# First products of a decoder layer taken by k-tile over both token tiles, with x loaded in smaller pieces

## The chip, the core and the metric

The kernel runs on one core of a Trainium2 chip. The metric is the time of one execution on the device in microseconds (us); a lower time is better. Five engines run their own instruction lists side by side and wait for each other through semaphores: TensorE (PE, matrix products; PEld is its loading of the stationary operand), VectorE (DVE), ScalarE (ACT), GpSimd (POOL) and SyncE (SP, which here only issues DMA transfers). Each list is worked through in the order in which it was written.

## What is computed

One layer of a decoder over 256 tokens of width 1024 in float32: a half-step feed-forward block with SwiGLU, two token mixers that share one input projection, and a second half-step feed-forward block, each followed by a layer norm. The part that matters here is the first feed-forward block:

```python
def swiglu(x, w_up, w_down):
    gate, up = jnp.split(x @ w_up, 2, axis=-1)
    return (jax.nn.silu(gate) * up) @ w_down

x = layer_norm(ALPHA * x + 0.5 * swiglu(x, ffn1_w_up[l], ffn1_w_down[l]), ln1_g[l], ln1_b[l])
```

x is 256 x 1024, w_up is 1024 x 5632 and w_down is 2816 x 1024.

## The kernel before

**Products in three passes.** Each float32 operand is split into a high part of type fp32r (a cast, on ACT) and a low part, the operand less its high part (a subtraction, on DVE). A product of a k-tile (128 rows of the contraction) is three matmuls that add up in one bank of PSUM: high x high, high of x with low of w, low of x with high of w. `passes` (L119) writes these three, and all of them are recorded on L117.

**Tokens** come in two tiles of 128 rows, t = 0 and t = 1. x has to stand transposed for the products: a block of 128 x 128 is transposed by TensorE (L190) into a bank of PSUM, four blocks to a bank, and `split` takes high (L203, ACT) and low (L204, DVE) out of that bank into the tile `X`. `XT(key, t, src, half)` does this for one token tile and half of the 1024 columns.

**Weights** come in units of 1 MB. A unit has a `raw` tile, which the DMA fills (L865), and two tiles `S` for its high part (cast on ACT, L875) and low part (subtraction on DVE, L878). There are three `raw` buffers, and the load of a further unit waits until the last low part of the unit that held its buffer is made. The first two units, columns 0 to 255 of gate and up for all of k, are loaded and split in four chunks of 128 x 512 each: a chunk is one k-tile, so unit 0 holds k = 0 to 3 and unit 1 holds k = 4 to 7. Later units are split in two chunks of 128 x 1024.

**The first products** are the 48 matmuls that `rows_both` (L316) writes: 8 k-tiles x 3 passes x 2 token tiles into one bank for each token tile. The order is half by half and in each half token tile by token tile: k = 0 to 3 of t = 0, k = 0 to 3 of t = 1, then k = 4 to 7 of t = 0 and of t = 1. The transposes of x stand ahead of them and between them: x of t = 0, columns 0 to 511, first; after 6 products x of t = 1, columns 0 to 511; after 12 and 18 products the two other halves. When a bank is full, `U_epi` takes it on (Silu on ACT, L391, and a product on DVE, L392). Behind the 48 stand the column units (`U_cols`), in which the weights are the stationary operand: eight products of 512 columns with the high part, of which the first four read the unit's first chunk, and eight of 256 columns with the low part.

**Ahead of the products** TensorE multiplies zeros from the tile `still`: `idle(6)` before the first transposes and `idle(3)` after them (L147).

**What sets the order.** All engines' lists are written by one walk over TensorE's operations (L913 on), which keeps a clock of its own, one column of a product at 1/2400 us. Before each operation `advance` (L890) decides whether chunks of weights are split now: a chunk that the operation's unit needs is always written first, whole unit by whole unit; further chunks when their due time is less than a lead ahead, no sooner after the chunk before than a pace allows, and not in a `quiet` time. `prep` (L870) writes the cast on ACT and the subtraction on DVE. What follows an operation (the split of a bank of transposes, Silu) is written right behind it, so casts of weights and casts of x stand on ACT's list in the order of this walk.

**Loads.** `load` (L860) issues the transfers of the weights on SP. Between the chunks of unit 0 it puts x: chunks 0 and 1, then x of t = 1 columns 0 to 511, chunks 2 and 3, then the two other halves of x. x of t = 0, columns 0 to 511, is issued by ACT as its first instruction.

## Time and profile before

| | us |
|---|---|
| median of three runs | 647.35 (646.94 to 647.46) |
| the profiled execution | 647.14 |
| its span, from the first to the last instruction | 645.1 |
| PE busy | 635.1, 3440 matmuls |
| DVE busy | 449.9 |
| ACT busy | 354.8 |

A profile has one row for an instruction, or for a run of equal ones (x6 is six of them, and the duration then goes from the start of the first to the end of the last). Times are counted from the span's start. The bracket at the end of a row says how long the engine stood idle before it and what ended that. Matmuls overlap: the next one starts before the row of the last has ended, so that the distance of their starts is the time that one costs. The span and the time outside it (2.0 us) make the time of the execution.

### The profile page before, as it was taken

The numbers are of one execution on the slowest core, as the hardware profiler recorded it, in microseconds if no ns is written. First come the engines' busy times: TensorE is split into PE (matmuls) and PEld (weight loads), VectorE is DVE, ScalarE is ACT, GpSimd is POOL, SyncE is SP. The second block draws the span as 40 slices with busy tenths as digits, with TensorE's granted clock in tenths as the row PEclk, the third lists the DMA queues.
The fourth block names the chain that finished last, engine by engine and source line by source line (L and its number), as shares of the span: only waits on it lengthen the run. The fifth ranks groups of instructions, "written<-read, shape, count | busy, mean of one in ns | idle before, by whom it ended". The sixth has DMA issues, their size and how long they took to land.

```text
span 645.1 us, 8783 instructions
## 1 busy us (share of the span) xinstructions
PE 635.1 (98%) x3440; PEld 548.6 (85%) x3440; DVE 449.9 (70%) x707; ACT 354.8 (55%) x608; POOL 18.6 (3%) x27
## 2 busy tenths in 40 slices
PE   8999999999999999999999999999999999999995
PEld 6888888888888888898888888888888888888884
DVE  4776666656678676777659898886866666666636
ACT  5665555555534558667678665552555555555510
POOL 2000000000011000000000000001100000000002
PEclk9999999999999999999999999999999999999999
DMA  8866666668636573546647656572565755555301
GB/s 292 284 207 199 221 226 202 199 203 274 193 113 192 156 216 97 185 134 206 186 139 215 234 196 195 196 253 75 195 194 203 257 196 196 196 196 195 131 2 65
DMA packets 95854, 121.18 MB, mean 188 GB/s; under 512 B 2197, under 2 KB 84421, under 8 KB 95813
## 3 DMA queue, kind: packets, MB, share of 16 engines
q1 hardware_dynamic: 95668, 120.36, 57.4%
q8 instruction: 27, 0.44, 0.3%
q10 hardware_dynamic: 144, 0.26, 0.1%
q14 instruction: 15, 0.11, 0.1%
HBM read 119.56 MB, written 1.05 MB: 187 GB/s over the span
## 4 chain that ended last, share of the span: by engine, by line
PE 97%; DMA 1%; POOL 0%; DVE 0%; SPq 0%; issue 0%; ACT 0%; POOLq 0%
PE acc L117 96%; PE acc L190 1%; DMA raw<-in_ffn_w_up 1%; SPq L865 0%; POOL rs L250 0%; POOL nmr L812 0%; DVE S L878 0%; ACT S L875 0%; SPq L106 0%; POOLq L944 0%; POOL N L815 0%; DVE bn L240 0%; DVE N L238 0%; DVE mv L246 0%; PE acc L707 0%
## 5 line engine op out<-in xcount | busy, mean ns | idle before, releaser
L117 PE MATMUL acc<-X,S 128*128 128x512 f32 (+1 forms) x2368 | 420.8, 338 | 0.0
L117 PEld LDWEIGHTS acc<-X,S 128*128 128x128 f32 x2368 | 364.3, 189 | 48.8
L878 DVE TENSOR_TENSOR S<-raw,S 128x1024 fp32r<-128x1024 f32 (+1 forms) x224 | 267.9, 1205 | 40.9 <-ACT S L875 39.7
L875 ACT CAST S<-raw 128x1024 fp32r<-128x1024 f32 (+1 forms) x224 | 227.9, 1035 | 47.3 <-PE acc L117 41.2
L117 PE MATMUL acc<-S,T 128*128 128x512 f32 (+1 forms) x546 | 123.7, 383 | 0.0
L117 PEld LDWEIGHTS acc<-S,T 128*128 128x128 f32 x546 | 100.1, 188 | 19.5
L376 DVE TENSOR_TENSOR T<-T,acc 128x256 f32<-128x256 f32 x124 | 52.0, 419 | 85.4 <-ACT T L375 85.3
L375 ACT COPY T<-acc 128x256 f32<-128x256 f32 x124 | 46.0, 371 | 101.7 <-PE acc L117 100.8
L117 PE MATMUL acc<-S,X 128*128 128x512 f32 x336 | 80.3, 394 | 0.9 <-ACT S L875 0.5
L117 PEld LDWEIGHTS acc<-S,X 128*128 128x128 f32 x336 | 62.1, 188 | 14.4 <-DVE S L878 1.2
L213 ACT CAST T<-T 128x256 fp32r<-128x256 f32 x38 | 15.5, 407 | 23.0 <-DVE T L427 23.0
L203 ACT CAST X<-acc 128x512 fp32r<-128x512 f32 (+1 forms) x24 | 12.4, 516 | 26.9 <-PE acc L190 13.7
L204 DVE TENSOR_TENSOR X<-acc,X 128x512 fp32r<-128x512 f32 (+1 forms) x24 | 14.3, 598 | 14.9 <-ACT X L203 14.9
L421 ACT ACTIVATE T<-T 128x256 f32<-128x256 f32 x38 | 15.9, 419 | 11.6 <-DVE T L376 11.6
L238 DVE SCALAR_TENSOR_TENSOR N<-acc,N 128x512 f32<-128x512 f32 (+1 forms) x13 | 8.4, 643 | 15.8 <-PE acc L117 15.8
L250 POOL TENSOR_TENSOR rs<-ve,mhalf 128x1 f32<-128x1 f32 x6 | 5.8, 964 | 460.5 <-DVE ve L248 460.5
L208 DVE TENSOR_TENSOR T<-T,T 128x256 fp32r<-128x256 f32 x38 | 15.9, 419 | 4.4 <-ACT T L213 4.4
L427 DVE TENSOR_TENSOR T<-T 128x256 f32<-128x256 f32 x38 | 16.2, 425 | 1.3
L376 DVE TENSOR_TENSOR N<-N,acc 128x256 f32<-128x256 f32 x24 | 10.1, 419 | 9.3 <-ACT N L375 9.1
L375 ACT COPY N<-acc 128x256 f32<-128x256 f32 x24 | 8.8, 367 | 8.4 <-PE acc L117 8.2
L203 ACT CAST T<-acc 128x128 fp32r<-128x128 f32 (+1 forms) x20 | 7.0, 350 | 7.8 <-PE acc L190 4.0
L204 DVE TENSOR_TENSOR T<-acc,T 128x128 fp32r<-128x128 f32 (+1 forms) x20 | 7.9, 395 | 4.5 <-ACT T L203 4.5
(71 smaller groups left out, 204.8 us busy)
## 6 DMA issues: line engine op xcount, KB each, us to landing
raw<-in_ffn_w_up SPq DMA_DIRECT2D x38, 1024.0 KB, 5.1
raw<-in_w_in SPq DMA_DIRECT2D x32, 1024.0 KB, 5.5
raw<-in_ffn_w_down SPq DMA_DIRECT2D x22, 1024.0 KB, 4.9
raw<-in_w_proj_attn SPq DMA_DIRECT2D x4, 1024.0 KB, 5.6
raw<-in_w_proj_conv SPq DMA_DIRECT2D x4, 1024.0 KB, 4.9
raw<-in_w_out SPq DMA_DIRECT2D x4, 1024.0 KB, 5.0
raw<-in_ffn_w_up SPq DMA_DIRECT2D x8, 512.0 KB, 5.0
raw<-in_ffn_w_up SPq DMA_DIRECT2D x8, 256.0 KB, 5.4
```

The lines of the kernel that those rows point to most:

```text
L117: return Op(lambda: nc.tensor.matmul(dst(), lhsT=lhsT(), rhs=rhs(), start=start, stop=stop), cols, unit)
L203: nc.scalar.copy(hi, src)
L204: nc.vector.tensor_tensor(lo, src, hi.bitcast(F), op=OP.subtract)
L208: nc.vector.tensor_tensor(lo, src, hi.bitcast(F), op=OP.subtract)
L213: nc.scalar.copy(hi, src)
L238: nc.vector.scalar_tensor_tensor(y[:, c], src, scale, st["ax", t][:, c], op0=OP.mult, op1=OP.add)
L375: nc.scalar.copy(dst, bank[:, 256:512])
L376: nc.vector.tensor_tensor(dst, dst, bank[:, 0:256], op=OP.add)
L421: defer(0.8, lambda: nc.scalar.activation(g[:, 0:256], g[:, 0:256], AF.Silu))
L427: nc.vector.tensor_tensor(g[:, 0:256], g[:, 0:256], g[:, 256:512], op=OP.mult)
L875: nc.scalar.copy(u.hi[:, s], u.raw[:, s])
L878: nc.vector.tensor_tensor(u.lo[:, s], u.raw[:, s], u.hi[:, s].bitcast(F), op=OP.subtract)
```

## The change

`rows_both` gets a written order, `seq`, of products (token tile, k-tile, which passes) and of transposes. The products run k-tile by k-tile, both token tiles at each, so that the k-tiles of unit 0 are used up after 24 products and not after the half of one token tile. Each operation also carries the number of its chunk, and `advance` writes only those chunks ahead of it that it needs, no longer the whole unit. Until the fourth split of x is written, `state["quiet"]` is set to 1e9, which keeps chunks from being written ahead of need; after it, to 0. The first chunk alone is written early, by `more`, behind the second group of idle products.

x comes in five pieces in place of four: columns 0 to 255 of t = 0 by ACT, then, each behind one of the four chunks of unit 0 on SP, columns 256 to 511 of t = 0, columns 0 to 511 of t = 1, and the two other halves. `x_first` takes the place of `XT` for x. The first piece is cast and subtracted by DVE alone (`by_dve`); the second one by ACT and DVE in one step of 2 blocks; the third one in two steps of 2 blocks; the last two in one step of 4 blocks. The idle products are 4 and 2 in place of 6 and 3.

```diff
-    load_x(0, 0, nc.scalar)
+    load_x(0, 0, 2, nc.scalar)
...
+    def x_first(t, k, n, done, evac):
+        def out_(bank):
...
+            evac(lambda i, m: (xT[:, k + i:k + i + m, 0, t, :], xT[:, k + i:k + i + m, 1, t, :],
+                               bank.rearrange("p (k n) -> p k n", k=4)[:, i:i + m]))
+            if done:
+                make_ax(t, st["x", t])
+                N.free()
+        return transposes(lambda i: st["x", t][:, (k + i) * 128:(k + i + 1) * 128], n, out_)
...
-    early = {1: [(1, 0)], 3: [(0, 1), (1, 1)]}
+    early = {0: (0, 2, 2), 1: (1, 0, 4), 2: (0, 4, 4), 3: (1, 4, 4)}
...
-    add(idle(6))
-    add(xts[0, 0])
-    add(idle(3))
-    base[-1].after.append(T.free)
-    e0, e1 = ffn("x", a["ffn1_w_up"][0], a["ffn1_w_down"][0], 1, 1,
-                 {6: [xts[1, 0]], 12: [xts[0, 1]], 18: [xts[1, 1]]}, 3, lambda t: ln_fin(t, 1))
+    def by_dve(part):
+        hi, lo, src = part(0, 2)
+        nc.vector.tensor_copy(hi, src)
+        nc.vector.tensor_tensor(lo, src, hi.bitcast(F), op=OP.subtract)
+    def by_both(part, n=4, w=4):
+        for i in range(0, n, w):
+            split(*part(i, w))
+    def open_up():
+        state["quiet"] = 0.0
+    ALL, HI, LO = ((0, 0), (0, 1), (1, 0)), ((0, 0), (1, 0)), ((0, 1),)
+    state["quiet"] = 1e9
+    add(idle(4))
+    add(x_first(0, 0, 2, False, by_dve))
+    e0 = add(idle(2))
+    base[-1].after += [T.free, lambda: more()]
+    first = x_first(0, 2, 2, False, lambda part: by_both(part, 2, 2))
+    second = x_first(1, 0, 4, False, lambda part: by_both(part, 4, 2))
+    third, fourth = (x_first(t, 4, 4, True, by_both) for t in range(2))
+    fourth[-1].after.append(open_up)
+    seq = [first, (0, 0, HI), (0, 0, LO), (0, 1, HI), second, (0, 1, LO), (1, 0, HI[:1]), (1, 1, HI[:1]), (1, 0, LO), (1, 1, LO),
+           (1, 0, HI[1:]), (1, 1, HI[1:]), (0, 2, ALL), third, (1, 2, ALL), (0, 3, ALL), fourth, (1, 3, ALL)]
+    seq += [(t, k, ALL) for k in range(4, KT) for t in range(2)]
...
-            if must is None or pos[id(must)] < state["prep"]:
+            p = -1 if must is None else pos[id(must)]
+            if p < state["prep"] or p == state["prep"] and part is not None and part < c:
```

ACT's list from its first cast to the first Silu. Names: `raw` to `S` is the high part of a chunk of weights, `acc` to `X` the high part of transposed x, `T` from `acc` the Silu. Before:

```order
L203 CAST X_115<-acc_110 128x4x128
L875 CAST S_122<-raw_88 128x512 x4
L203 CAST X_115<-acc_141 128x4x128
L875 CAST S_154<-raw_96 128x512
L203 CAST X_115<-acc_158 128x4x128
L875 CAST S_154<-raw_96 128x512 x2
L203 CAST X_115<-acc_178 128x4x128
L875 CAST S_154<-raw_96 128x512
L875 CAST S_199<-raw_101 128x1024 x2
L391 ACTIVATE T_217<-acc_132 128x256
```

The four chunks of unit 0 stand in a row, ahead of the second piece of x. The same place after the change:

```order
L916 CAST S_118<-raw_88 128x512
L208 CAST X_112<-acc_122 128x2x128
L916 CAST S_118<-raw_88 128x512
L208 CAST X_112<-acc_135 128x2x128 x2
L916 CAST S_118<-raw_88 128x512
L208 CAST X_112<-acc_157 128x4x128
L916 CAST S_118<-raw_88 128x512
L208 CAST X_112<-acc_176 128x4x128
L916 CAST S_185<-raw_97 128x512 x4
L916 CAST S_217<-raw_102 128x1024
L413 ACTIVATE T_225<-acc_127 128x256
L413 ACTIVATE T_231<-acc_145 128x256
```

Chunks of unit 0 and pieces of x now alternate, and the second chunk of the first column unit (`S_217`) has moved behind both Silus.

TensorE's list from the third group of transposes on (`acc_158` and `acc_157`), to the first products of unit 1. `S_122` and `S_118` are the high part of unit 0, `S_154` and `S_185` that of unit 1, `S_155` and `S_186` its low part. Before:

```order
L190 MATMUL acc_158<-ident,N_82 128x128 x4
L117 MATMUL acc_167<-S_122,X_115 128x512
L117 MATMUL acc_167<-S_123,X_115 128x512
L117 MATMUL acc_167<-S_122,X_115 128x512 x2
L117 MATMUL acc_167<-S_123,X_115 128x512
L117 MATMUL acc_167<-S_122,X_115 128x512
L190 MATMUL acc_178<-ident,N_83 128x128 x4
```

After:

```order
L195 MATMUL acc_157<-ident,N_82 128x128 x4
L118 MATMUL acc_145<-S_118,X_112 128x512
L118 MATMUL acc_145<-S_119,X_112 128x512
L118 MATMUL acc_145<-S_118,X_112 128x512
L118 MATMUL acc_127<-S_118,X_112 128x512
L118 MATMUL acc_127<-S_119,X_112 128x512
L118 MATMUL acc_127<-S_118,X_112 128x512
L195 MATMUL acc_176<-ident,N_83 128x128 x4
L118 MATMUL acc_145<-S_118,X_112 128x512
L118 MATMUL acc_145<-S_119,X_112 128x512
L118 MATMUL acc_145<-S_118,X_112 128x512
L118 MATMUL acc_127<-S_185,X_112 128x512
```

Before, six products of t = 1 (`acc_167`) on chunks 0 and 1 stand between the two groups of transposes. After it, three products of t = 1 on chunk 2 and three of t = 0 (`acc_127`) on chunk 3 stand there, and the first product of unit 1 comes three products behind the last group of transposes.

## Rows read from the trace of the kernel before

**Rows 1.** The page's first part (busy time of each engine and its share of the span), and its fourth, the shares of each engine in the chain that ended last.

```profile
PE 635.1 (98%) x3440; PEld 548.6 (85%) x3440; DVE 449.9 (70%) x707; ACT 354.8 (55%) x608; POOL 18.6 (3%) x27
...
PE 97%; DMA 1%; POOL 0%; DVE 0%; SPq 0%; issue 0%; ACT 0%; POOLq 0%
```

**Rows 2.** That chain in order of time: start, us, what it ran through (x is the number of instructions).

```profile
2.69 4.72 DMA raw<-in_ffn_w_up
...
7.44 0.63 ACT S L875
...
8.09 0.70 DVE S L878
...
12.54 9.37 PE acc L117 x45
...
25.37 164.20 PE acc L117 x864
```

**Rows 3.** Busy time by stretch (PE, PEld, DVE, ACT, POOL, each with its number of instructions), then the granted TensorE clock (1.00 is 2.4 GHz), the DMA engines' busy share and GB/s.

```profile
5.40:8.00 2.60, 1.81 (x7) 1.22 (x8) 1.87 (x3) 1.60 (x3) 0.00 (x0) 1.00 1.01 350
8.00:12.30 4.30, 4.23 (x25) 3.25 (x24) 3.18 (x5) 3.02 (x7) 2.45 (x2) 1.00 1.05 351
12.30:19.20 6.90, 6.90 (x33) 5.72 (x32) 5.08 (x8) 4.16 (x7) 0.00 (x0) 1.00 1.10 350
...
36.00:300.00 264.00, 264.00 (x1440) 228.51 (x1439) 182.93 (x293) 150.93 (x264) 5.77 (x5) 1.00 0.59 190
300.00:637.00 337.00, 337.00 (x1833) 292.09 (x1832) 239.76 (x371) 181.12 (x305) 6.00 (x6) 1.00 0.55 180
```

**Rows 4.** The timeline of the first 30 us, TensorE's rows: start, us, line, operation, tiles, shape, number.

```profile
1.29 2.93 PE L147 MATMUL acc<-T 128*128 128x512 f32 x6 [1.29 <-POOL T L90]
...
4.02 0.66 PE L190 MATMUL acc<-ident,N 128*128 128x128 f32 x4
...
4.44 0.96 PE L147 MATMUL acc<-T 128*128 128x512 f32 x3
...
5.87 0.49 PE L117 MATMUL acc<-S,X 128*128 128x512 f32 x1 [0.48 <-ACT S L875]
...
6.68 1.42 PE L117 MATMUL acc<-S,X 128*128 128x512 f32 x5 [0.31 <-DVE S L878]
...
7.94 0.60 PE L190 MATMUL acc<-ident,N 128*128 128x128 f32 x4
...
12.30 7.08 PE L117 MATMUL acc<-S,X 128*128 128x512 f32 x30
...
19.21 2.70 PE L117 MATMUL acc<-X,S 128*128 128x512 f32 x15
```

**Rows 5.** The same timeline, ACT's rows.

```profile
4.72 0.59 ACT L203 CAST X<-acc 128x512 fp32r<-128x512 f32 x1 [2.10 <-PE acc L190]
...
5.20 1.35 ACT L875 CAST S<-raw 128x512 fp32r<-128x512 f32 x2
...
7.44 1.34 ACT L875 CAST S<-raw 128x512 fp32r<-128x512 f32 x2 [0.90 <-DMA raw<-in_ffn_w_up]
...
8.69 0.58 ACT L203 CAST X<-acc 128x512 fp32r<-128x512 f32 x1
...
15.70 2.00 ACT L875 CAST S<-raw 128x1024 fp32r<-128x1024 f32 x2 [2.01 <-DMA raw<-in_ffn_w_up]
...
17.60 0.38 ACT L391 ACTIVATE T<-acc 128x256 f32<-128x256 f32 x1
...
19.66 0.38 ACT L391 ACTIVATE T<-acc 128x256 f32<-128x256 f32 x1
```

**Rows 6.** ACT's timeline in the stretch from 5.83 to 6.6 us alone, which leaves the second of the two casts that start at 5.20.

```profile
5.92 0.62 ACT L875 CAST S<-raw 128x512 fp32r<-128x512 f32 x1
```

**Rows 7.** The same timeline as in rows 4 and 5, rows of DVE and one of POOL (its scaling of x for the residual).

```profile
5.34 0.69 DVE L204 TENSOR_TENSOR X<-acc,X 128x512 fp32r<-128x512 f32 x1 [5.34 <-ACT X L203]
...
8.98 2.45 POOL L268 TENSOR_SCALAR N<-N 128x1024 f32<-128x1024 f32 x2 [6.66 <-DMA N<-in_x]
...
11.10 0.86 DVE L878 TENSOR_TENSOR S<-raw,S 128x512 fp32r<-128x512 f32 x1 [0.99 <-ACT S L875]
...
12.49 1.28 DVE L878 TENSOR_TENSOR S<-raw,S 128x512 fp32r<-128x512 f32 x2
```

**Rows 8.** ACT's and DVE's instructions grouped by line and shape: number, busy us, mean ns of one, idle time before.

```profile
L203 ACT CAST X<-acc 128x512 fp32r<-128x512 f32 x16 | 9.4, 588 | 22.1 <-PE acc L190 13.7 <-PE acc L117 8.4
...
L203 ACT CAST X<-acc 128x256 fp32r<-128x256 f32 x8 | 3.0, 373 | 4.9 <-PE acc L117 4.9
...
L875 ACT CAST S<-raw 128x512 fp32r<-128x512 f32 x8 | 4.9, 620 | 2.3 <-DMA raw<-in_ffn_w_up 2.1
...
L204 DVE TENSOR_TENSOR X<-acc,X 128x512 fp32r<-128x512 f32 x16 | 10.9, 685 | 11.9 <-ACT X L203 11.9
...
L204 DVE TENSOR_TENSOR X<-acc,X 128x256 fp32r<-128x256 f32 x8 | 3.4, 424 | 2.9 <-ACT X L203 2.9
```

**Rows 9.** SP's timeline: the issue of transfers, first those at the start, then the first that had to wait for a buffer.

```profile
0.71 1.29 SPq L865 DMA_DIRECT2D raw<-in_ffn_w_up  x2
2.06 0.59 SPq L106 DMA_DIRECT2D N<-in_x  x1
...
9.54 0.45 SPq L865 DMA_DIRECT2D raw<-in_ffn_w_up  x1
```

More of the change, by code (lines that the diff above doesn't have):

```diff
@@ L36, in __init__ @@
     def __init__(self, fn, cols, unit=None):
-        self.fn, self.cols, self.unit, self.after = fn, cols, unit, []
+        self.fn, self.cols, self.unit, self.chunk, self.after = fn, cols, unit, None, []
 class Unit:
@@ L117, in mm, with passes @@
         return Op(lambda: nc.tensor.matmul(dst(), lhsT=lhsT(), rhs=rhs(), start=start, stop=stop), cols, unit)
-    def passes(dst, sta, mov, first, last, cols, unit=None):
-        return [mm(dst, lambda x=x: sta(x), lambda w=w: mov(w), first and i == 0, last and i == 2, cols, unit)
-                for i, (x, w) in enumerate(((0, 0), (0, 1), (1, 0)))]
+    def passes(dst, sta, mov, first, last, cols, unit=None, ends=None, which=((0, 0), (0, 1), (1, 0))):
+        ends = ends() if ends else [(first and i == 0, last and i == 2) for i in range(3)]
+        return [mm(dst, lambda x=x: sta(x), lambda w=w: mov(w), *ends[i], cols, unit)
+                for i, (x, w) in enumerate(which)]
     def add(ops):
@@ L314, in rows, with rows_both, first, fin @@
         return add(ops)
-    def rows_both(key, uns, epis, between):
-        box, ops = {}, []
-        for half in range(2):
-            for t in range(2):
-                for k in range(half * 4, half * 4 + 4):
-                    u = uns[half]
-                    ops += passes(lambda t=t: box[t], lambda s, k=k, t=t: st["xT", key][:, k, s, t, :],
-                                  lambda w, u=u, k=k: (u.hi, u.lo)[w][:, (k % 4) * 512:(k % 4 + 1) * 512],
-                                  k == 0, k == KT - 1, 512, u)
-        for t in range(2):
-            def first(t=t, f0=ops[12 * t].fn):
-                box[t] = ACC.get()
-                f0()
-            def fin(t=t):
-                epis[t](box[t])
-                ACC.free()
-            ops[12 * t].fn = first
-            ops[12 * t + 35].after.append(fin)
-        for i in range(len(ops)):
-            for extra in between.get(i, []):
-                add(extra)
-            add([ops[i]])
+    def rows_both(key, uns, epis, seq):
+        box, count = {}, {0: 0, 1: 0}
+        for item in seq:
+            if not isinstance(item, tuple):
+                add(item)
+                continue
+            t, k, which = item
+            u = uns[k // 4]
+            ops = passes(lambda t=t: box[t], lambda s, k=k, t=t: st["xT", key][:, k, s, t, :],
+                         lambda w, u=u, k=k: (u.hi, u.lo)[w][:, (k % 4) * 512:(k % 4 + 1) * 512],
+                         False, False, 512, u, lambda n=count[t], which=which: [(n + i == 0, n + i == 23) for i in range(len(which))],
+                         which)
+            for op in ops:
+                op.chunk = k % 4
+            if count[t] == 0:
+                def first(t=t, f0=ops[0].fn):
+                    box[t] = ACC.get()
+                    f0()
+                ops[0].fn = first
+            count[t] += len(which)
+            if count[t] == 3 * KT:
+                def fin(t=t):
+                    epis[t](box[t])
+                    ACC.free()
+                ops[-1].after.append(fin)
+            add(ops)
+        assert count == {0: 3 * KT, 1: 3 * KT}
         return len(base)
@@ L882, in prep, with more @@
         defer(DELAY if now["t"] > 12 else 0.0, rest, u)
+    def more():
+        u, c = order[state["prep"]], state["chunk"]
+        prep(u, c)
+        state["t"] = now["t"]
+        state["chunk"] += 1
+        if state["chunk"] == u.chunks:
+            state["prep"] += 1
+            state["chunk"] = 0
     def flush(must=None):
@@ L888, in flush, with advance @@
                 item[2]()
-    def advance(must=None):
+    def advance(must=None, part=None):
         flush(must)
@@ L903, in advance @@
                     break
-            prep(u, c)
-            state["t"] = t
-            state["chunk"] += 1
-            if state["chunk"] == u.chunks:
-                state["prep"] += 1
-                state["chunk"] = 0
+            more()
         flush(must)
@@ L914, in layer @@
         now["t"] = t
-        advance(op.unit)
+        advance(op.unit, op.chunk)
         op.fn()
```

17 lines of the change are left out of this document (10 added, 7 removed).

## The prediction

> **What bounds the kernel now.** I read the page's busy shares and the shares of the chain of waits first [rows 1]: PE is busy for 635.1 of 645.1 us and holds 97% of the chain that ended last. The windows [rows 3] say where the rest lies: from 36 to 300 us and from 300 to 637 us PE is busy all the time, 264.00 of 264.00 and 337.00 of 337.00. So nothing between 36 and 637 us can take up a delay or give back a gain: what the start of the kernel loses or wins goes through to the end one to one. The chain in order of time [rows 2] reaches back from 25.37 us through PE alone to some 8.8 us, and from there through a subtraction of DVE, a cast of ACT and the landing of chunk 2 at 7.42. The change lies wholly in this opening, so the question is when PE is done with the 48 first products and whether it can go on. Before, the first of them starts at 5.87 and the first product of the column units at 19.21 [rows 4]. A product costs 0.23 us (30 from 12.30 to 19.21), four transposes take 0.60 from the first start to the last end and some 0.45 of PE's time. 48 x 0.23 + 12 x 0.11 is 12.4 us of work in the 13.3 us from 5.87 to 19.21: the opening has only about 1 us of waiting in it, nearly all before 9 us, plus what an earlier start could bring.
>
> **The change part by part.**
>
> *Loads.* The same bytes come in the same order but for two places: half of the first piece of x moves behind chunk 0, and x of t = 0, columns 512 on, now stands ahead of chunk 3, which therefore lands one step later, long before ACT takes it up (below). Up to the end of chunk 1 there are 768 KB as before, and up to the ends of chunks 4 to 7 the same as before. One more issue on SP costs about 0.6 [rows 9], while the engines move 350 GB/s from 5.4 us on [rows 3], 0.75 us for 256 KB: the issues stay ahead. I take chunk 1 to be there at 5.92, when ACT cast it before [rows 6], and put 0.4 either way on that for the new order.
>
> *First piece by DVE alone, fewer idle products.* Before, ACT made x's cast at 4.72 and only then, at 5.20, chunk 0's [rows 5]. Now chunk 0's cast needs no turn behind x, and the first product can come 0.5 to 0.8 us earlier than 5.87. DVE's cast of 128x256 out of PSUM is in no row: between nothing and 0.69 (a whole subtraction of 128x512, [rows 7]), I take 0.4, by the subtraction of the same shape (0.42, [rows 8]). It is worth nothing at the end, because of what follows: PE's list then stands at the products of chunk 1, which comes at 5.92 as before. By 7.15 PE will have done five products; before, it had done six by 7.94 [rows 4].
>
> *The clock.* The six idle products took 2.93 us, the three behind the transposes 0.96 [rows 4], so TensorE reached the upper of its two levels, 2.4 GHz, around the transposes at 4.0, although the record reads 1.00. Now there are four and two idle products with transposes between. If the lower level lasted past 7 us, two products and four transposes in the chain below would take about 0.4 longer. I take nothing and keep 0.4 as a bound. (The Trainium skill, "TensorE: Matmul & The Clock Gate", Part 4, says that transposes do not count as activity for the clock; by it the 0.4 would be paid. In this trace the rise comes while transposes run, after 2.7 us of products, which leaves it open.)
>
> *The new order.* This is the part that costs. ACT's list before has all four chunks of unit 0 ahead of the second piece of x; now casts of chunks and of x alternate, and each cast of x waits for transposes which stand on PE's list behind products of the chunk before. So the chain goes round through PE, ACT and DVE once for each k-tile:
>
> Chunk 1 is cast from 5.92 to 6.54 (0.62, [rows 6]); PE starts 0.05 later (5.82 to 5.87, [rows 4, 5]) at 6.59, the next product 0.33 later (0.23, and 0.1 more behind a wait: five products in 1.42 at 6.68), the transposes of x of t = 1 at 7.15, done at 7.75. ACT: 0.04 and a cast of 128x256, 0.37 [rows 8], to 8.16. DVE: 0.03 and 0.42, to 8.61. ACT's second cast of 128x256 waits for that one, to 9.01. Chunk 2, landed at 7.42 or a little earlier, is cast behind it: it begins 0.09 before the end of the last, as ACT does at 8.69 [rows 5], and ends at 9.54. DVE 0.03 and 0.69 [rows 7], PE 0.05: the second product of k-tile 2, which needs the low part, starts at 10.31.
>
> From there one round is: 0.33 to the third product, 0.23 to the transposes, 0.60 for them, 0.04 and 0.59 for ACT's cast of x [rows 5, 8], 0.03, then DVE's subtraction for x and the one for the next chunk back to back, 1.28 for two [rows 7] (the next chunk's cast on ACT ends within the first of them), 0.05 to PE: 3.15 us. PE's own work in a round is six products and four transposes, 1.8 us, so that it stands idle for 1.35. Two rounds lie between k-tiles 2, 3 and 4: the second product of k-tile 4 starts at 16.61. With the last piece of x gone the chunks of unit 1 come 0.53 apart on ACT against 1.4 of products each, so the other 22 of the 24 products follow densely: 0.1 + 23 x 0.23 = 5.4, and the first column unit starts at 22.0 where it started at 19.21: **+2.8**.
>
> *The first column unit.* Before, both its casts were done by 17.70 [rows 5]. Now the second one, 1.04 us, stands behind the Silu of t = 1, which waits for the 48th product: 22.15 and 0.38, then the cast from 22.45 to 23.5. The unit's fifth product, due at 22.0 + 4 x 0.23 = 22.9, starts at 23.55 and pays the 0.1 of a wait: **+0.7**. If that cast were ready it would be 0.
>
> *Refill.* SP's first load that waits for a `raw` buffer was issued at 9.54 [rows 9], when unit 0's last low part was done; now that part ends at 13.4, so it goes 3.9 us later, and casts and subtractions of the next units move with it. The load before it ran to 15.70, which takes most of that. I follow the lists on with the same durations: one more wait of about **+0.4** at some 36 us, where DVE's subtraction of a chunk of w_down ends after it is due. Bounds 0 and 0.7.
>
> *POOL* scales x as before, once x has landed; while it ran, from 8.98 to 11.43, a subtraction on DVE took 0.86 in place of 0.69 [rows 7]. Two of DVE's steps in the chain may meet it: 0 to +0.35, I take 0.
>
> **Sum:** 2.8 + 0.7 + 0.4 = 3.9, about 4.0 with the small roundings upward. The profiled execution took 647.14 (span 645.1 and 2.0 around it), which gives 651.1; the median of the runs is 0.2 above that execution, so 651.2. Bounds: landings -0.4 to +0.4, clock to +0.4, refill -0.4 to +0.3, POOL to +0.35, hand-overs -0.3 to +0.3: 650.1 to 652.9.
>
> **The rivals.**
>
> *A, faster.* If ACT had chunks 2 and 3 cast while it waits for x, a round would cost PE's own 1.8 and the opening would be bound by PE from its first product on: 0.8 for the earlier start and 1.0 of the waiting before 9 us would be won, 645.5. It decides itself at a round of 1.8 us. Against it stand the lists, in which the cast of chunk 3 comes behind the cast of the x piece whose transposes come behind chunk 2's products. 4%.
>
> *B, no difference.* The rounds shrink to PE's own 1.8 (-2.7) and the Silu finds the column unit's second cast done (-0.7), but the start wins nothing: 0.6 is left, 647.9. 5%.
>
> *C, slower still: the clock falls.* From 8 to 17 us PE would stand idle for a third of the time in stretches of up to 0.8 us. Were the clock to go back to 1.2 GHz, products would cost about 0.43 (2.93 less the last one's tail, over the idle products, [rows 4]) and the 24 products of unit 1, which nothing hides, 24 x 0.2 = 4.8 more at worst, half of it if the clock comes back midway: 653.5 to 656. Before, PE stood idle for 0.48 and 0.31 us at 5.4 and 6.4 [rows 4] and the clock stayed at 1.00 [rows 3]. 6%. (The same page of the Trainium skill, "A second HAM failure mode: psum-queue depth-cycling", tells of a kernel whose clock swung because of short pauses between groups of products; no run here shows it.)
>
> **How the numbers follow.** The forecast, slower by 4, has 85%; A 4%, B 5%, C 6%. A measurement of this kernel can tell about 0.2%, 1.3 us, from no change. Slower by more than that: the forecast and C, 0.90, taking off a little for a forecast gone wrong in size; the same 0.06; faster 0.04. The range leaves out A, B and C (15%) and takes in the bounds of the sum with some room below for waits that I count twice: 649.4 to 652.9.
>
> **What would show it.** In the profile after: ACT's casts of chunks 2 and 3 start some 1.5 and 3 us after landing, each right behind a cast of x; PE has gaps of 0.5 to 0.8 us about 10, 12.5, 13.3, 15.5 and 16.3 us; rounds of 3.1 to 3.2 us; the first column product starts at 22.0 and its unit has a gap of about 0.7 behind four products. The forecast is wrong if that start lies before 20.5, if PE waits anywhere between 40 and 637 us, or if the clock reads less than 1.00 behind 5 us.

## The result and the profile after

The changed kernel takes **652.38 us** (median of 4 runs, 651.55 to 653.21) against 647.26 (646.94 to 647.46, 4 runs): ratio 1.0079, 95% interval 1.0067 to 1.0092. It is 5.1 us slower; 651.2 was forecast, with a range up to 652.9. The four runs form two pairs, 651.55 and 651.60 (span 649.8) and 653.17 and 653.21 (span 651.4), and the median is the mean of one run of each. The profiled execution is the 653.21 one, so its trace is of the upper pair.

Windows of the changed kernel, columns as in [rows 3]; the column ahead of the DMA share is the granted clock:

```profile
5.40:8.00 2.60, 1.39 (x5) 0.48 (x3) 1.20 (x3) 0.84 (x2) 0.00 (x0) 0.97 0.93 296
8.00:10.00 2.00, 1.96 (x8) 1.22 (x7) 0.38 (x2) 0.37 (x1) 0.31 (x1) 0.50 1.00 306
10.00:12.00 2.00, 2.00 (x7) 1.54 (x7) 1.47 (x3) 0.89 (x2) 1.78 (x2) 0.68 1.07 375
12.00:14.00 2.00, 1.76 (x10) 1.23 (x9) 0.54 (x1) 0.21 (x1) 0.00 (x0) 1.00 1.08 356
14.00:19.20 5.20, 3.61 (x14) 1.92 (x14) 2.91 (x5) 3.14 (x7) 0.00 (x0) 1.00 0.82 265
...
36.00:300.00 264.00, 264.00 (x1436) 228.28 (x1435) 185.18 (x294) 151.07 (x264) 5.76 (x5) 1.00 0.59 193
300.00:643.00 343.00, 343.00 (x1869) 297.50 (x1868) 244.88 (x382) 185.63 (x314) 6.00 (x6) 1.00 0.55 180
```

Behind 36 us PE is busy all the time, as before, so the loss lies ahead of it. In [rows 3] PE stood still for 0.8 us from 5.4 to 8 us and for 0.07 from 8 to 12.3; now for 1.2 from 5.4 to 8 us and for 1.6 from 14 to 19.2. And from 8 to about 11 us the granted clock reads 0.50, the lower of its two levels (1.2 GHz), which no row of before shows.

PE's timeline, columns as in [rows 4]; L118 and L195 are the lines that were L117 and L190:

```profile
5.07 1.23 PE L118 MATMUL acc<-S,X 128*128 128x512 f32 x3
7.51 0.94 PE L118 MATMUL acc<-S,X 128*128 128x512 f32 x2 [1.21 <-ACT S L916]
8.24 1.11 PE L195 MATMUL acc<-ident,N 128*128 128x128 f32 x4
9.00 3.34 PE L118 MATMUL acc<-S,X 128*128 128x512 f32 x8
12.59 0.73 PE L118 MATMUL acc<-S,X 128*128 128x512 f32 x2 [0.24 <-DVE S L919]
...
15.75 0.73 PE L118 MATMUL acc<-S,X 128*128 128x512 f32 x2 [0.31 <-DVE S L919]
...
18.92 5.51 PE L118 MATMUL acc<-S,X 128*128 128x512 f32 x23 [0.31 <-DVE S L919]
24.27 1.07 PE L118 MATMUL acc<-X,S 128*128 128x512 f32 x4
25.85 2.00 PE L118 MATMUL acc<-X,S 128*128 128x512 f32 x11 [0.51 <-ACT S L916]
...
31.07 17.27 PE L118 MATMUL acc<-X,S 128*128 128x512 f32 x96
48.18 5.62 PE L118 MATMUL acc<-S,T 128*128 128x512 f32 x24
```

The first product starts 0.8 earlier than in [rows 4], and then PE waits 1.21 us for chunk 1. The rounds stand out: second products of k-tiles 2, 3 and 4 at 12.59, 15.75 and 18.92, 3.16 and 3.17 apart. The first column product comes at 24.27 (19.21 in [rows 4]), and behind four of them PE waits for ACT's cast.

ACT's and SP's timelines, which answer to [rows 5, 6] and [rows 9], and the rows of DVE and POOL that answer to [rows 7]:

```profile
6.84 0.62 ACT L916 CAST S<-raw 128x512 fp32r<-128x512 f32 x1 [1.21 <-DMA raw<-in_ffn_w_up]
...
10.25 0.37 ACT L208 CAST X<-acc 128x256 fp32r<-128x256 f32 x1 [0.49 <-DVE X L209]
10.52 0.62 ACT L916 CAST S<-raw 128x512 fp32r<-128x512 f32 x1
13.79 0.59 ACT L208 CAST X<-acc 128x512 fp32r<-128x512 f32 x1 [2.65 <-PE acc L195]
14.27 0.62 ACT L916 CAST S<-raw 128x512 fp32r<-128x512 f32 x1
```

```profile
0.72 0.66 SPq L906 DMA_DIRECT2D raw<-in_ffn_w_up  x1
1.43 0.57 SPq L107 DMA_DIRECT2D N<-in_x  x1
2.06 0.55 SPq L906 DMA_DIRECT2D raw<-in_ffn_w_up  x1
2.65 0.60 SPq L107 DMA_DIRECT2D N<-in_x  x1
```

```profile
11.17 1.36 DVE L919 TENSOR_TENSOR S<-raw,S 128x512 fp32r<-128x512 f32 x1
```

```profile
10.95 1.05 POOL L273 TENSOR_SCALAR N<-N 128x1024 f32<-128x1024 f32 x1 [0.21 <-DMA N<-in_x]
```

Chunk 1 is cast at 6.84, not at 5.92 as in [rows 6]; its transfer is issued at 2.06, where the two first chunks were issued in one go from 0.71 to 2.00 [rows 9]. Chunks 2 and 3 are cast right behind a cast of x, 1.7 and 4.1 us after they landed (8.8 and 10.2, by the time from issue to landing). And one subtraction on DVE takes 1.36 us in place of 0.69, beside a scaling on POOL.

**The span, term by term** (this profile less the one of before, whose rows behind 25 us are these):

```profile
25.12 17.00 PE L117 MATMUL acc<-X,S 128*128 128x512 f32 x96
41.97 5.62 PE L117 MATMUL acc<-S,T 128*128 128x512 f32 x24
```

To the first column product: 24.27 - 19.21 = 5.06. From the column start to the 96 products of the column units behind: 6.80 (24.27 to 31.07) where it was 5.91 (19.21 to 25.12): 0.89. The 96 products: 17.11 (31.07 to 48.18) where it was 16.85 (25.12 to 41.97): 0.26. From there to the end 603.2 and 603.1. Sum 6.3, the difference of the spans, 651.4 and 645.1.

**Time outside the span** is not the same in all kernels. It is 2.0 us in the kernel before and 1.8 in each run of the changed kernel, so the two profiled executions differ by 6.1, not 6.3. In the experiments below the medians are 1.8 (one chunk ahead, cast ahead of the Silu, scalings written later, loads of before, three parts undone), 2.0 (the two with only loads changed) or 2.1 to 2.2 (the other five). No row shows what makes the difference; a difference of up to 0.4 us between the times of two of these kernels can come from there.

### The profile page after: what moved, and what is told of

The parts are those of the page before. It is cut to its first block, busy times and chain, and to the rows that moved or that the text cites. A ratio compares the mean times of both kernels' runs of the same rounds, so it can differ in the third digit from the quotient of the medians.

```text
span 651.4 us, 8783 instructions
## 1 busy us (share of the span) xinstructions
PE 638.6 (98%) x3437; PEld 548.6 (84%) x3437; DVE 451.5 (69%) x710; ACT 354.3 (54%) x609; POOL 18.3 (3%) x27
## 4 chain that ended last, share of the span: by engine, by line
PE 96%; DMA 1%; DVE 1%; ACT 1%; issue 0%; POOL 0%; SPq 0%; POOLq 0%; DVEq 0%
PE acc L118 95%; PE acc L195 1%; DMA raw<-in_ffn_w_up 1%; DVE S L919 0%; ACT S L916 0%; ACT X L208 0%; POOL rs L255 0%; POOL nmr L853 0%; SPq L906 0%; SPq L107 0%; DVE X L209 0%; POOLq L991 0%; POOL N L856 0%; DVE bn L245 0%; DVE N L243 0%
## 5 line engine op out<-in xcount | busy, mean ns | idle before, releaser
L118 PE MATMUL acc<-X,S 128*128 128x512 f32 (+1 forms) x2368 | 421.4, 338 | 0.5 <-ACT S L916 0.5
L118 PEld LDWEIGHTS acc<-X,S 128*128 128x128 f32 x2368 | 364.4, 190 | 49.9 <-ACT S L916 0.9
L118 PE MATMUL acc<-S,T 128*128 128x512 f32 (+1 forms) x546 | 123.8, 383 | 0.0
L118 PEld LDWEIGHTS acc<-S,T 128*128 128x128 f32 x546 | 100.1, 188 | 19.5
L118 PE MATMUL acc<-S,X 128*128 128x512 f32 x336 | 83.1, 400 | 3.1 <-ACT S L916 2.2
L118 PEld LDWEIGHTS acc<-S,X 128*128 128x128 f32 x336 | 62.5, 190 | 18.5 <-ACT S L916 3.4
L208 ACT CAST X<-acc 128x512 fp32r<-128x512 f32 (+1 forms) x25 | 12.3, 492 | 32.3 <-PE acc L195 18.5
```

Source lines behind the costliest of these rows:

```text
L118: return Op(lambda: nc.tensor.matmul(dst(), lhsT=lhsT(), rhs=rhs(), start=start, stop=stop), cols, unit)
L208: nc.scalar.copy(hi, src)
```

## The experiments

Each run had the kernel before on the same chip beside it, 647.16 to 647.68 in the median; "above before" is measured against that one. "Column start" is the first column product in the run's own trace (before: 19.21).

### One chunk ahead

```diff
         advance(op.unit, op.chunk)
+        if op.chunk is not None:
+            k = pos[id(op.unit)] * 4 + op.chunk
+            while 2 <= k < 7 and state["prep"] * 4 + state["chunk"] < k + 2:
+                more()
```

From k-tile 2 on, the chunk behind the one that is needed is split too, so ACT has it before it turns to the next piece of x.

> The changed kernel, but from k-tile 2 on the chunk after the one that a product needs is split right with it, so that on ACT the cast of chunk 3 stands ahead of the third piece of x and that of chunk 4 ahead of the fourth. Theory (the round through PE, ACT and DVE of 3.16 us costs 1.35 per k-tile): the two rounds shrink to nearly PE's own 1.8, 2.5 to 2.9 us come off, 649.2 to 650.2 where the changed kernel took 652.4. Rival (the late landing of chunk 1 and the fall of the clock make the loss, and the waits in the rounds would only move to another place): less than 0.8 comes off, 651.6 to 652.4.

Measured: 649.55 us (649.40 to 650.69), 1.0036 [1.0023, 1.0048], 1.9 above before; column start 20.51. The rounds, PE's rows:

```profile
11.52 0.73 PE L118 MATMUL acc<-S,X 128*128 128x512 f32 x2 [0.23 <-DVE S L919]
12.09 0.60 PE L195 MATMUL acc<-ident,N 128*128 128x128 f32 x4
12.44 1.63 PE L118 MATMUL acc<-S,X 128*128 128x512 f32 x6
13.91 0.60 PE L195 MATMUL acc<-ident,N 128*128 128x128 f32 x4
14.27 6.41 PE L118 MATMUL acc<-S,X 128*128 128x512 f32 x27
```

From 12.09 to 13.91 is one round: 1.82 us, the 1.8 of PE's own work, where it was 3.16. That is the time and the round that the theory of the rounds gave. From the second product of k-tile 2 to the column start it takes 8.99 us (11.52 to 20.51) in place of 11.68 (12.59 to 24.27), so both rounds lost 1.3. A round's waiting is the turn of the chunk's cast behind the cast of x, as the prediction had it, and neither the transposes nor the change between the two accumulators.

### The column unit's cast ahead of the Silu

```diff
             sc = T.get()
+            if key == "x" and t == 0:
+                more()
             nc.scalar.activation(sc[:, 0:256], bank[:, 0:256], AF.Silu)
```

> The changed kernel, but the second cast of the first column unit stands ahead of the two Silus on ACT. Theory: the gap of 0.67 us behind four products of that unit goes and a little of the wait behind it, 0.7 to 0.9 off, 651.5 to 651.8. Rival (the low part of the same chunk on DVE, or a later unit, is late next): 0 to 0.3 off.

Measured: 651.01 us (650.74 to 651.15), 1.0053 [1.0040, 1.0067]. The gap behind four column products is gone:

```profile
23.13 2.97 PE L118 MATMUL acc<-X,S 128*128 128x512 f32 x15
```

From the column start to the end of the span it takes 649.4 - 23.13 = 626.3; in the changed kernel 651.4 - 24.27 = 627.1, before 645.1 - 19.21 = 625.9. So this cast is worth 0.8 of the 1.2 that lie behind the column start, the later 0.26 included (the 96 products take 16.84 here). The time lies below the range of the theory: in this trace the opening is shorter too, the column start comes 1.14 earlier than in the profile of the changed kernel, with the subtraction for chunk 2 at 0.69 and the clock at 1.00.

### POOL's scalings written later

```diff
-                make_ax(t, st["x", t])
-                N.free()
+                def late():
+                    make_ax(t, st["x", t])
+                    N.free()
+
+                defer(20.0, late)
```

> The changed kernel, but POOL's two scalings of x are written 20 us later, away from the opening. Theory (they hold up DVE's subtraction for chunk 2, 1.36 us where others take 0.69, and PE waits for just that one): 0.5 to 0.8 off, 651.6 to 651.9, and the subtraction takes 0.69. Rival (that subtraction is hidden, or is long for another reason): 0 off.

Measured: 652.11 us (651.53 to 652.26), 1.0068 [1.0055, 1.0081]. As a test this missed: POOL has nothing else on its list, so the scalings ran at 9.20 and 10.92 as ever; only their place in the program moved. But its trace (span 649.8, as in the lower pair of the changed kernel) shows the chain undisturbed: chunk 1 cast at 6.60, clock 1.00 throughout, the subtraction for chunk 2 from 10.27 in 0.69, the second product of k-tile 2 at 11.01, column start 22.69.

### Six and three idle products

```diff
-    add(idle(4))
+    add(idle(6))
...
-    e0 = add(idle(2))
+    e0 = add(idle(3))
```

> The changed kernel with 6 and 3 idle products as before the change in place of 4 and 2. Theory 1 (the clock fell to 0.50 from 7.9 to 11.3 us because too little ran just before, and the idle products would fill it): the clock stays at 1.00, 0.7 to 1.6 off, 650.8 to 651.7, and the spread between runs goes from 1.6 us to under 0.6. Theory 2 (the empty stretch from 5.8 to 7.5 us, where PE waits for chunk 1, decides, and idle products ahead of it do nothing): the clock falls again in some runs, 652.4 to 652.7.

Measured: 652.60 us (652.33 to 652.70), 1.0078 [1.0065, 1.0090]. The clock is 1.00 throughout in the trace and the runs lie within 0.4 of each other, where the changed kernel's spread over 1.7. But nothing is gained in the level: the spans, 650.1 to 650.6, lie between the two pairs of the changed kernel, and the time outside the span is 0.4 longer. There is no trace of the other runs. So this doesn't show that the fall of the clock is what separates the two pairs.

### The loads of before

```diff
-    load_x(0, 0, 2, nc.scalar)
+    load_x(0, 0, 4, nc.scalar)
...
-    early = {0: (0, 2, 2), 1: (1, 0, 4), 2: (0, 4, 4), 3: (1, 4, 4)}
+    early = {1: [(1, 0, 4)], 3: [(0, 4, 4), (1, 4, 4)]}
...
```

> New order and first piece as in the changed kernel, x loaded as in the kernel before (256 KB for the first piece on ACT's queue, the other three behind chunks 1 and 3). Theory (the new places and sizes of the loads of x are why chunk 1 lands at 6.4 to 6.8 us in place of 5.9, and this goes to the end): chunk 1's cast starts at 5.9 to 6.0, the second product of k-tile 2 at 10.3 to 10.4 if the clock stays up, first column product at 22.0; time 650.7 to 651.0, and 652.4 where the clock falls. Rival (chunk 1 lands late for another reason, or its landing is hidden): 651.5 to 651.7, and 653.2 where the clock falls.

Measured: 651.26 us (651.10 to 652.14), 1.0066 [1.0054, 1.0079], 4.1 above before. Chunk 1 is cast at 5.92 again, but four of the five runs take 651.10 to 651.46, between the theory's 650.7 to 651.0 and the rival's 651.5. The trace (of the slowest run) says what came late instead:

```profile
5.27 2.55 PE L118 MATMUL acc<-S,X 128*128 128x512 f32 x5
7.62 0.78 PE L195 MATMUL acc<-ident,N 128*128 128x128 f32 x4
...
11.62 0.73 PE L118 MATMUL acc<-S,X 128*128 128x512 f32 x2 [0.86 <-DVE S L919]
```

```profile
10.22 1.34 DVE L919 TENSOR_TENSOR S<-raw,S 128x512 fp32r<-128x512 f32 x1
```

The first five products take 2.55 us in a row, some 0.43 from one to the next, the spacing of the idle products at the start; the granted clock reads 1.00 there all the same. The transposes come at 7.62, not 7.15, and end 0.65 late; then the subtraction for chunk 2 is 0.65 longer. 10.31 + 0.65 + 0.65 is 11.61: all of the lateness of that product.

### The new loads alone, in the kernel before

```diff
-    load_x(0, 0, nc.scalar)
+    load_x(0, 0, 2, nc.scalar)
...
-    early = {1: [(1, 0)], 3: [(0, 1), (1, 1)]}
+    early = {0: (0, 2, 2), 1: (1, 0, 4), 2: (0, 4, 4), 3: (1, 4, 4)}
...
```

> The kernel before with nothing but the loads of the changed kernel. Theory (the new loads bring chunk 1 later by 0.6 to 0.8): chunk 1's cast at 6.5 to 6.7 in place of 5.92; ACT has its chunks in a row there, so all else shifts: 648.7 to 649.5 against 647.3. Rival 1 (loads cost nothing by themselves): 647.3. Rival 2 (chunk 1 lands as before and only the first transposes wait for the second half of the piece): 648.0.

Measured: 649.42 us (648.90 to 651.38), 1.0040 [1.0026, 1.0054], 2.3 above before; column start 21.52, 2.3 later. The slowest run has a mean clock of 0.993, as the profiled run of the changed kernel, and no trace. ACT's rows (L875 is the cast of a chunk, as in [rows 5]):

```profile
6.75 0.62 ACT L875 CAST S<-raw 128x512 fp32r<-128x512 f32 x1 [0.37 <-DMA raw<-in_ffn_w_up]
9.03 0.62 ACT L875 CAST S<-raw 128x512 fp32r<-128x512 f32 x1 [1.66 <-DMA raw<-in_ffn_w_up]
10.42 0.62 ACT L875 CAST S<-raw 128x512 fp32r<-128x512 f32 x1 [0.78 <-DMA raw<-in_ffn_w_up]
```

Chunk 1 comes 0.8 later than in [rows 6], chunk 2 1.6 later than in [rows 5]. The loads cost more by themselves than any part of the changed kernel that I had priced except the rounds.

### The second half piece on ACT's queue

```diff
     load_x(0, 0, 2, nc.scalar)
+    load_x(0, 2, 2, nc.scalar)
...
-    early = {0: (0, 2, 2), 1: (1, 0, 4), 2: (0, 4, 4), 3: (1, 4, 4)}
+    early = {1: (1, 0, 4), 2: (0, 4, 4), 3: (1, 4, 4)}
...
```

(against the kernel of the last experiment)

> As loads_alone (the kernel before with the loads of the changed kernel), but the second half of the first piece of x is issued by ACT's queue behind the first half, so that SP's list has no issue between chunk 0 and chunk 1 any more; the sizes and the place of the other pieces stay. Theory (what delays is the turn on SP's list: every load behind it is issued 0.6 us later): chunk 1 lands at 5.9 to 6.2 in place of 6.73, x of t = 1 at 6.7 to 7.0 in place of 8.32, chunk 2 at 7.4 to 7.8 in place of 9.00, time 647.2 to 648.0. Rival (the two small pieces themselves make the engines slower): landings as in loads_alone, 649.2 to 649.5.

Measured: 648.55 us (647.97 to 649.45, 11 runs), 1.0021 [1.0012, 1.0029], 1.3 above before, in two groups about 648.0 and 649.2. SP's and ACT's rows:

```profile
0.71 1.29 SPq L866 DMA_DIRECT2D raw<-in_ffn_w_up  x2
2.06 0.59 SPq L106 DMA_DIRECT2D N<-in_x  x1
```

```profile
6.19 1.14 ACT L876 CAST S<-raw 128x512 fp32r<-128x512 f32 x2
7.68 0.62 ACT L876 CAST S<-raw 128x512 fp32r<-128x512 f32 x1 [0.35 <-DMA raw<-in_ffn_w_up]
```

The same two half pieces of x, and chunk 1 is there when ACT wants it, chunk 2 at 7.68 against 9.03 and 7.44 [rows 5]. So it was the turn on SP's list that made the chunks late, not the size of the pieces. The time was forecast too low: in this trace, of the upper group, the first product comes only at 6.86, a microsecond behind [rows 4], since the first four transposes wait for the second half piece (landed at 4.9, on SP's queue at 4.5), and six products take 3.31 us, the later ones 0.43 apart. Of the 2.3 that the loads cost, the other queue gave back 1.0.

### The order of before, with the new loads and first piece

```diff
...
-    seq += [(t, k, ALL) for k in range(4, KT) for t in range(2)]
+    seq = [first, (0, 0, ALL), (0, 1, ALL), second, (0, 2, ALL), (0, 3, ALL), third, (1, 0, ALL), (1, 1, ALL), fourth, (1, 2, ALL), (1, 3, ALL)]
+    seq += [(t, k, ALL) for t in range(2) for k in range(4, KT)]
...
-        advance(op.unit, op.chunk)
+        advance(op.unit)
```

> Loads, first piece and idle products of the changed kernel; the order of the 48 products of the kernel before (four k-tiles of one token tile, then four of the other), and all chunks of unit 0 split ahead as before. Theory (loads and order are what costs; the order some 2 to 2.7 of it): 648.7 if chunk 1 lands at 5.9, 650.0 if it lands at 6.6, first column product 1.4 to 2.8 later than 19.21. Rival (the order is all of the loss, loads and first piece nothing): 647.3, first column product at 19.2.

Measured: 650.12 us (649.70 to 650.54), 1.0047 [1.0034, 1.0060], 3.0 above before; column start 21.95, chunk 1 cast at 6.46. So of the 5.1 of the change, 3.0 are there without its order.

### Three parts undone, the order kept

```diff
+            if key == "x" and t == 0:
+                more()
...
-    load_x(0, 0, 2, nc.scalar)
+    load_x(0, 0, 4, nc.scalar)
...
+            while 1 <= k < 7 and state["prep"] * 4 + state["chunk"] < min(k + 2, 8):
+                more()
```

(with the table of loads of before)

> The k-tiles still run over both token tiles and DVE alone splits the first piece; but ACT casts chunks 2 to 4 ahead of the x piece that it cast before them (from k-tile 2 on, one chunk ahead), the second cast of the first column unit stands ahead of the Silu, and x is loaded as before. Theory (these three are the whole loss, 2.0 + 0.6 to 0.7 + 0.7 to 0.9 of the 4.3 from 647.3 to 651.6, refill goes with them): 647.3 to 648.3, first column product at 19.2 to 20.0. Rival (products of both tiles by turns cost by themselves, some 1 or more, through transposes between them): 648.7 or more.

Measured: **647.11 us** (646.64 to 647.38, 11 runs), 0.9997 [0.9988, 1.0006], the time of before; column start 19.25:

```profile
13.00 6.41 PE L118 MATMUL acc<-S,X 128*128 128x512 f32 x27
19.25 2.97 PE L118 MATMUL acc<-X,S 128*128 128x512 f32 x15
```

The k-tiles run over both token tiles here, by the changed kernel's own table, and DVE alone splits the first piece. Together they cost nothing measurable, and gain nothing.

### POOL's scalings held behind the Silus

```diff
             st["h", j, t] = sc
+            if key == "x" and j == 0:
+                nc.gpsimd.tensor_copy(late, sc[:, 0:1])
+                make_ax(t, st["x", t])
+                N.free()
```

(with the loads of before; the scalings in the first transposes are taken out)

> As old_loads, but POOL's two scalings of x wait for the Silus of the first products (by a copy of one column of their result, one element for each partition), so that none runs before 22 us. Theory (a scaling on POOL beside DVE's subtraction for chunk 2 doubles that one from 0.69 to 1.34, which the chain pays in full): the subtraction takes 0.69 in the profile, second product of k-tile 2 at 10.9 to 11.0 in place of 11.62, first column product at 22.6 to 22.7 in place of 23.31, time 651.1 to 651.3 in each run and none at 652. Rival (POOL is not the reason): the subtraction takes 1.3 again, or the times lie from 651.1 to 652.1 as in old_loads.

Measured: 652.20 us (651.69 to 652.76), 1.0076 [1.0062, 1.0090]: the time missed by 1, though the chain did what was expected. DVE's rows:

```profile
9.89 0.69 DVE L921 TENSOR_TENSOR S<-raw,S 128x512 fp32r<-128x512 f32 x1
...
23.87 1.95 DVE L921 TENSOR_TENSOR S<-raw,S 128x1024 fp32r<-128x1024 f32 x1 [0.51 <-ACT S L918]
```

The subtraction for chunk 2 takes 0.69, the second product of k-tile 2 starts at 10.63, the column start is 22.32, the earliest of the kernels with the change's rounds. But POOL's second scaling now runs from 23.70 to 24.74, and the subtraction of the first column unit takes 1.95 where the same one took 1.23 in the kernel with the loads of before. PE waits 0.55 for it, and from the column start to the end it takes 627.8, with the loads of before alone 627.0 (650.3 - 23.31). The collision was moved, not removed. Another 0.4 of the missed 1 lies outside the span (2.1 against 1.8).

### Six and three idle products with the loads of before

> As old_loads, but with six and three idle products, as in the kernel before. In old_loads the products came 0.43 apart up to 7.6 us, and the transposes for the second token tile started at 7.62 in place of the 7.15 worked out for products 0.23 apart. Theory (fewer idle products, a later rise of the clock, 0.5 to 0.65 us in the chain): products 0.23 to 0.24 apart from 6.6 us on at the latest, the transposes at 7.2 to 7.4, the second product of k-tile 2 at 10.4 to 10.6 where POOL doesn't meet DVE (11.1 to 11.3 where it does), time 650.7 to 651.0. Rival (the rise does not hang on them, or the later first product takes the gain): 651.2 to 651.6.

The edit is the two lines shown above, with the loads of before. Measured: 652.50 us (651.47 to 653.05), 1.0079 [1.0066, 1.0091]; the theory's gain isn't there. The products do come 0.23 to 0.34 apart (three in 1.06), but the transposes for the second token tile start at 7.47 all the same (7.62 in the kernel with the loads of before). Chunk 1 wasn't late: issued at 1.43, it landed at 5.2. ACT takes it up only a microsecond after that, behind the second piece of x:

```profile
5.95 0.37 ACT L208 CAST X<-acc 128x256 fp32r<-128x256 f32 x1 [0.68 <-PE acc L195]
6.22 0.62 ACT L916 CAST S<-raw 128x512 fp32r<-128x512 f32 x1
```

That piece is cast at 5.95 and not at 5.65, since the idle products hold up its transposes (first product at 5.67 in place of 5.27). So what the closer products gain, the later start of the opening takes, as the rival said. In the last experiment, with four and two, the transposes start at 7.46, there because chunk 1 landed at 6.2. From there on the two traces are alike up to 9.89, where the subtraction for chunk 2 starts in both:

```profile
9.89 1.51 DVE L919 TENSOR_TENSOR S<-raw,S 128x512 fp32r<-128x512 f32 x1
```

```profile
8.81 2.06 POOL L273 TENSOR_SCALAR N<-N 128x1024 f32<-128x1024 f32 x2 [6.49 <-DMA N<-in_x]
```

1.51 with POOL at work, 0.69 without; second product 11.46 and 10.63, column start 23.15 and 22.32. One difference in the opening, 0.83 us, carried whole to the column start.

### All of these together

> As parts_undone (647.11, and 0.45 between its two groups of runs), with six and three idle products and POOL's scalings of x behind the Silus. Theory (both still cost there: POOL met the subtraction for chunk 3, 1.52 in place of 0.69, and five products came 0.43 to 0.6 apart): 646.2 to 646.7, half a microsecond and more below the kernel before. Rival (what the opening gains there is taken by the later first product or by loads): 646.9 to 647.3.

The three parts undone, six and three idle products, and POOL behind the Silus. Measured: 647.97 us (647.26 to 648.51, 11 runs), 1.0009 [1.0000, 1.0018]. No gain: 0.7 above before, where the three parts alone were level with it (0.9 between the two medians, which are of different chips). Column start 19.29; POOL's two scalings, now beside the column units, make PE wait 0.20 for a subtraction up to 21.70, and the spans of the two profiles, 645.6 and 645.4, differ by as much. Another 0.4 lies outside the span (2.2 against 1.8 in every run); where the rest comes from stays open. No version here beats the kernel before.

## Why the prediction was right, and where its sum was off

**The median lies in the range, in part by luck.** The upper pair, 653.17 and 653.21, lies above 652.9; three runs of that kind out of four would have put the median outside. Of the prediction's own signs the rounds, the gap behind four column products and the chunks' casts behind casts of x came true, but the column start is 24.27 and not 22.0, and the clock read less than 1.00 behind 5 us, which it had named as a sign of being wrong.

**The mechanism and its two main numbers held.** A round was forecast at 3.15 us and took 3.16 and 3.17; from the second product of k-tile 4 to the column start 5.4 was forecast and 5.35 came. The experiment with one chunk ahead brings the round down to PE's own 1.8 by taking away just the turn that the prediction named.

**Behind the column start the sum held too.** +0.7 for the column unit's cast and +0.4 for the refill; measured 0.89 and 0.26. The first is shown by taking the cast ahead of the Silu. Of the second no single gap is to be seen; the 96 products are longer as a whole, and the experiment that removes the first term removes this one as well, so it is not a cost of its own.

**Ahead of the rounds three terms were mis-sized,** each by more than its own bound. The second product of k-tile 2 was forecast at 10.31 and came at 12.59 in this trace:

- *Landing of chunk 1*, taken at 5.92 with "0.4 either way": +0.92. The step that failed is "the issues stay ahead". Each load on SP's list goes out 0.6 us later, and from 4 to 5 and from 5 to 6 us the DMA engines moved 146 and 172 GB/s, where it was 262 and 261 before; chunk 1, right behind the added issue, pays. That the issue is the cause is shown by moving it to ACT's queue (323 and 274 GB/s); why 0.6 of issue became 0.9 of landing isn't. In the seven kernels with these loads chunk 1 lands at 6.4 to 6.8 and is cast at 6.46 to 6.84. In the five with the loads of before and the new first piece it lands at 5.1 to 6.2 and is cast at 5.92 to 6.25, in three of them straight behind a cast of x and not at the landing. So a bound of 0.4 would have done for the loads of before, and not for these.
- *The clock*, "I take nothing": +0.68 in this trace. From the first product of chunk 1 to the transposes it took 0.73 in place of 0.56, and the four transposes 1.11 in place of 0.60. This is a small form of rival C, ahead of the products that it was priced for: the clock was back at 1.00 from 12 us on. It is in this trace alone of the thirteen of changed kernels as a granted clock under 0.90 in a window of the opening; the products 0.43 apart up to 7.6 or 10 us, at a reading of 1.00, are in others. A mean clock of 0.993 or 0.994, as in this run, stands beside runs without a trace of two kernels with these loads and the order of before (one of the new loads alone, three of the order of before with the new loads and first piece), so the fall may not hang on the new order.
- *POOL*, "0 to +0.35, I take 0": +0.67. The bound was read off one row, 0.86 in place of 0.69 [rows 7], as if each meeting cost that much. It is a wait for the end of POOL's instruction (below), so its price is set by how the two happen to start: 0.65 to 0.83 in the four traces of changed kernels in the table below.

0.92 + 0.68 + 0.67 = 2.27, the lateness of the column start (24.27 against 22.0). In the trace of the kernel with POOL's scalings written later, which I take to stand for the lower pair because its span is the same, only the landing is left: chunk 1 0.68 late, second product 0.70 late, column start 22.69, 0.7 late. The forecast then misses the lower pair by 0.4 and the upper one by 2.0. That clock and POOL lift the second run of the upper pair as well is argued, not shown: it has no trace, and its mean clock (0.996) is that of the lower pair.

**"This is the part that costs", said of the new order, is only half of it.** With the loads of before the order (with the first piece by DVE and four and two idle products) costs 4.1 us, what the sum said (4.0). That it is 4.1 by the same terms isn't shown: the one trace is of the slowest run, where the column start alone is 4.1 late, 1.3 of it by slow products and POOL. But loads and first piece cost 3.0 with the order of before, and all together 5.1, not 7.1. The parts hide each other: the order makes ACT wait with chunk 2 up to 10.5 us, and so hides that it lands at 8.8; the late chunk 1 hides that the first products can run 0.43 apart (with POOL's scalings written later three take 1.52, and PE still waits 0.77 for chunk 1). Which part "is" the loss depends on which one is undone first; undone together, nothing is left (647.11).

**The first piece by DVE** was forecast to bring the first product 0.5 to 0.8 earlier and to be worth nothing. It came 0.8 earlier (5.07), and PE then waited 1.21 for chunk 1. Right on both.

**Rival A**, that the rounds would fall to 1.8, was rightly held unlikely. What it needs is the extra line of the first experiment, and even then chunk 1 bounds the start; with the loads mended too the kernel gets back to 647.1 and not to 645.5.

## What to carry to other kernels

Where a list alternates between two kinds of work, cost the round that goes through all engines, and check whether the next piece can be prepared before the engine turns to the other kind: a few lines that cast one chunk ahead took 1.3 us out of each round. An added issue on a loading queue can be paid by the loads behind it (here 0.6 us of issue, and a chunk 0.9 late); on another queue the chunks came in time again, but the piece itself came later, so look at what waits for that too. And undo the parts of a slow change together as well as one by one: here each part hid some of the others' price. Before a difference of a few tenths is given to a cause, compare the spans as well as the times.

## What was not expected of the hardware

**DVE and POOL shut each other out.** DVE's subtraction of two SBUF operands and POOL's scaling don't share, one waits for the other. In five traces the subtraction of 128x512 that started while a scaling ran ended 0.53 to 0.54 behind that scaling's end:

| trace | subtraction | scaling's end | behind it |
|---|---|---|---|
| before [rows 7] | 11.10 to 11.96 | 11.43 | 0.53 |
| after | 11.17 to 12.53 | 12.00 | 0.53 |
| loads of before | 10.22 to 11.56 | 11.02 | 0.54 |
| three parts undone | 10.34 to 11.86 | 11.32 | 0.54 |
| idle products and loads | 9.89 to 11.40 | 10.87 | 0.53 |

So it does nearly all its 0.69 of work after POOL is done. Where DVE starts first POOL waits: in the kernel with the new loads alone its two scalings took 2.84 in place of 2.06, while the subtractions took 0.69 to 0.74. The subtraction with a PSUM operand isn't touched: in the kernel with three parts undone it took 0.43 at 9.82, in the middle of a scaling. The Trainium skill, "SBUF — State Buffer", section "SBUF: two separate sides", says this: DVE instructions with two SBUF inputs and GpSimd's that read SBUF share a pair of ports under an exclusive lock, and whoever starts first holds it for the whole instruction. The runs agree. The 0.15 by which the wait is shorter than the whole 0.69 isn't explained.

**The spacing of the products says more than the granted clock.** Five products that took 2.55 us stand under a reading of 1.00 in the kernel with the loads of before, and 1.42 under the same reading before [rows 4]. When the faster spacing begins varied from 4.4 us (before) to later than 10 us (half piece on ACT's queue); more idle products brought it forward with the loads of before, and didn't with the new ones (five products in 2.13 us), where it cost nothing because chunk 1 was late. The Trainium skill, "TensorE: Matmul & The Clock Gate", Part 4, says that transposes don't count as a busy TensorE in the same way; with two and two transposes among six idle products the late rise fits that, but no run here separates the transposes from the smaller number of idle products. What made the clock fall in the one trace stays open as well: PE had waited 1.21 us just ahead of it, and in the kernel with one chunk ahead it waited 1.01 at the same place and kept its clock.
